# Storing the last five tiles of a log-softmax in transfers of unequal numbers of partitions

## The chip, the cores and the metric

Every run uses one core of a Trainium2 chip; the experiments ran on three chips, each beside the kernel before on the same chip. The metric is the device time of one execution in microseconds (us). All runs here are fast, with a granted clock of 1.0.

## The reference

```python
def setup_inputs():
    batch, seq, vocab = 16, 512, 50000
    return {"x": np.random.randn(batch, seq, vocab).astype(np.float32)}

def reference(x):
    max_x = np.max(x, axis=-1, keepdims=True)
    shifted = x - max_x
    log_sum_exp = np.log(np.sum(np.exp(shifted), axis=-1, keepdims=True))
    return (shifted - log_sum_exp).astype(np.float32)
```

1,638.4 MB are read and as many written.

## The kernel before

A tile is 16 rows of x, each cut into 8 pieces: 128 partitions of 6,250 floats (25,000 B). There are 512 tiles in 64 rounds of 8 buffers. SP loads a buffer when its earlier store has landed; VectorE takes the maximum, ScalarE the exponentials with their sums, VectorE subtracts in place, and ScalarE issues the store. "Tile 507" is buffer 3 of the last round, "tile 511" the very last.

```python
P = 128
NBUF = 8

def take(engine, sem):
    engine.wait_ge(sem, 16).then_inc(sem, -16)

# SP
for j in range(NBUF):
    sync.dma_start(out=bufs[j], in_=dram(xq, 0, j)).then_inc(landed[j], 16)
with sync.Fori(1, rounds) as q:
    for j in range(NBUF):
        take(sync, stored[j])
        sync.dma_start(out=bufs[j], in_=dram(xq, q, j)).then_inc(landed[j], 16)
for j in range(NBUF):
    take(sync, stored[j])

# ... VectorE: front(j) waits for landed[j], takes the maximum; back(j) sums and subtracts

# ScalarE
def back(q, j):
    subtracted.next(
        scalar.dma_start(out=dram(oq, q, j), in_=bufs[j])
    ).then_inc(stored[j], 16)

# ... round 0
with scalar.Fori(1, rounds) as q:
    last = q - 1
    for j in range(NBUF):
        log((j - 1) % NBUF)
        front(j)
        back(q if j else last, (j - 1) % NBUF)
    settle()
log(NBUF - 1)
back(rounds - 1, NBUF - 1)
```

## Time and profile before

| | before |
|---|---|
| time, median | 7614.19 us (7613.91 to 7614.76, 4 runs) |
| VectorE, ScalarE busy | 79%, 41% |
| DMA | 430 GB/s over the span; 432 in the middle, 373 in the last fortieth |
| last increment of the last store | 7611.20 us after the start of the trace |

The lines themselves stand in the prediction. "DMA share" is the busy time of the 16 DMA engines, "GB/s" what they moved; a packet is counted whole in the stretch in which it starts. Two more things come from the trace's own records and from no view: the durations of single DMA packets (one row of 25,000 B is one packet), and the times at which each engine adds its increment to the semaphore of a transfer. The spread of the 16 increments of one transfer shows how far apart the engines are; how late the last one is, I call the lag of the slow engine.

### The profile page before, as it was taken

To read this page: it belongs to the slowest core of one execution; us is meant where nothing else is said; L and a number is where in the kernel's file an instruction comes from. 1 tells how busy PE (TensorE), PEld (TensorE's weight loads), DVE (VectorE), ACT (ScalarE), POOL (GpSimd) and SP (SyncE) were. 2 spreads that over 40 slices of the span, in tenths; PEclk is the share of its full clock that TensorE was granted. 3 is DMA by queue.
4 is the path that set the end of the run, shared out by engine and by line. 5 is a ranking of instruction groups with operands and counts; after the bars stand their busy time and mean duration, and the time that the engine had idled before them with its cause. 6 is when DMAs were issued, how large, how long until landed. Compare 5 with 4: busy or idle time off the path is not lost. (4 is left out here: it accounts for less than half of the span.)

```text
span 7612.6 us, 13283 instructions
## 1 busy us (share of the span) xinstructions
DVE 6049.3 (79%) x5632; ACT 3113.4 (41%) x2561; POOL 0.2 (0%) x4
## 2 busy tenths in 40 slices
DVE  8777877777777778777787777877777877778777
ACT  4444444444444443444444444444444444444443
POOL 0000000000000000000000000000000000000000
DMA  9999999999999999999999999999999999999998
GB/s 425 432 432 432 432 432 432 432 432 432 432 432 433 432 432 433 432 432 433 432 432 433 432 432 432 432 433 432 432 433 432 432 432 432 432 432 432 432 432 373
DMA packets 147459, 3276.89 MB, mean 430 GB/s; under 512 B 16384, under 2 KB 16384, under 8 KB 16384
## 3 DMA queue, kind: packets, MB, share of 16 engines
q1 hardware_dynamic: 73728, 1638.43, 50.0%
q10 hardware_dynamic: 73728, 1638.43, 50.0%
q14 instruction: 3, 0.02, 0.0%
HBM read 1638.40 MB, written 1638.40 MB: 430 GB/s over the span
## 5 line engine op out<-in xcount | busy, mean ns | idle before, releaser
L144 DVE TENSOR_REDUCE own<-buf 128x1 f32<-128x6250 f32 x512 | 3411.7, 6663 | 1267.0 <-DVEq L43 1267.0
L179 ACT ACTIVATE dump<-buf,negmax 128x3125 f32<-128x3125 f32 x1024 | 2929.3, 2861 | 33.3 <-DVE negmax L140 16.8
L188 ACT ACTIVATE logsum<-total 128x1 f32<-128x1 f32 x512 | 103.8, 203 | 4447.9 <-DVE total L140 4447.9
L153 DVE TENSOR_SCALAR buf<-buf,negmax,logsum 128x6250 f32<-128x6250 f32 x512 | 1810.2, 3536 | 138.9 <-ACT logsum L188 138.9
L126 DVE STREAM_TRANSPOSE block<-own 128x32 f32<-128x32 f32 x1024 | 216.6, 212 | 35.1
L129 DVE TENSOR_REDUCE rowval<-block 128x4 f32<-128x32 f32 x1024 | 190.4, 186 | 35.4
L135 DVE COPY spread<-rowval 128x32 f32<-128x32 f32 x1024 | 185.5, 181 | 35.6
L179 ACT ACTIVATION_READ_ACCUMULATOR dump<-buf,negmax 128x1 f32 x1024 | 190.8, 186 | 0.0
L140 DVE STREAM_TRANSPOSE total<-spread 128x32 f32<-128x32 f32 x512 | 108.4, 212 | 17.7
L140 DVE STREAM_TRANSPOSE negmax<-spread 128x32 f32<-128x32 f32 x512 | 108.3, 212 | 17.7
L149 DVE TENSOR_REDUCE own<-part 128x1 f32<-128x2 f32 x512 | 57.5, 112 | 2.4 <-ACT dump L179 2.4
L200 ACT ACT_TABLE_LOAD x1 | 1.3, 1283 | 0.9 <-SPq L85 0.9
L231 POOL MEMSET const-bfloat16-1.0<- 128x1 bf16 x1 | 0.1, 102 | 0.0
L231 POOL MEMSET const-uint8-127<- 128x1 uint8 x1 | 0.1, 102 | 0.0
L231 POOL MEMSET const-float32-0.0<- 128x1 f32 x1 | 0.1, 99 | 0.2 <-issue 0.2
L231 POOL MEMSET const-float32-1.0<- 128x1 f32 x1 | 0.1, 99 | 0.0
## 6 DMA issues: line engine op xcount, KB each, us to landing
buf<-in_x_dram SPq DMA_DIRECT2D x512, 3125.0 KB, 55.5
out_dram<-buf ACTq DMA_DIRECT2D x512, 3125.0 KB, 35.7
```

What stands on the lines that cost most here:

```text
L126: vector.transpose(out=block32, in_=own.to_broadcast([P, SQ]))
L129: vector.tensor_reduce(out=rowval, in_=block32.rearrange("p (r g) -> p r g", g=G), op=op, axis=AX, negate=negate,)
L135: vector.tensor_copy(out=spread.rearrange("p (r g) -> p r g", g=G), in_=rowval[:, :, None].to_broadcast([P, SQ // G, G]),)
L140: on_dve.next(vector.transpose(out=out, in_=spread)).then_inc(done.sem)
L144: vector.reduce_max(out=own, in_=bufs[j], axis=AX).then_inc(on_dve.sem)
L149: vector.tensor_reduce(out=own, in_=parts[j], op=ALU.add, axis=AX)
L153: vector.tensor_scalar(out=bufs[j], in0=bufs[j], scalar1=shift[j][:, 0:1], scalar2=logs[j], op0=ALU.add, op1=ALU.subtract,)
L179: ins = scalar.activation(out=dump, in_=bufs[j][:, c * EXP_C : (c + 1) * EXP_C], func=ACT.Exp, bias=shift[j][:, 0:1], scale=1.0, accum_out ...
L188: scalar.activation(out=logs[j], in_=totals[j][:, 0:1], func=ACT.Ln)
L200: nc.scalar.preload_act_table_set("natural_log_exp_and_others")
L231: nc = _bacc.Bacc("TRN2", target_bir_lowering=False, num_devices=1)
```

## The change

The intent is to even out the end: one of the 16 DMA engines has fallen behind, so the last five tiles are cut into transfers that should give it less, and others more. ScalarE's last round is taken out of its loop so that its stores can differ.

```diff
+SPLIT = (120, 8)
+STEPS = (*range(2, 16), 9)
+
+def groups(j):
+    return STEPS if j == NBUF - 1 else SPLIT if j >= NBUF - 5 else (P,)
+
-def take(engine, sem):
-    engine.wait_ge(sem, 16).then_inc(sem, -16)
+def take(engine, sem, n=16):
+    engine.wait_ge(sem, n).then_inc(sem, -n)
@@ SP
-            take(sync, stored[j])
+            take(sync, stored[j], 16 * len(groups(j)))
@@ ScalarE
-        def back(q, j):
-            subtracted.next(
-                scalar.dma_start(out=dram(oq, q, j), in_=bufs[j])
-            ).then_inc(stored[j], 16)
+        def back(q, j, groups=(P,)):
+            p = 0
+            for n in groups:
+                dst = dram(oq, q, j)
+                ins = scalar.dma_start(out=dst[p : p + n], in_=bufs[j][p : p + n])
+                if p == 0:
+                    subtracted.next(ins)
+                ins.then_inc(stored[j], 16)
+                p += n
+            assert p == P
@@
-        with scalar.Fori(1, rounds) as q:
+        with scalar.Fori(1, rounds - 1) as q:
             ...
+        for j in range(NBUF):
+            log((j - 1) % NBUF)
+            front(j)
+            back(rounds - 1 if j else rounds - 2, (j - 1) % NBUF, groups(j - 1))
         log(NBUF - 1)
-        back(rounds - 1, NBUF - 1)
+        back(rounds - 1, NBUF - 1, groups(NBUF - 1))
```

## The prediction

The forecast's sum, with all its terms: 7611.2 - 2.5 - 3.1 + 7.5 = 7613.1, and 3.0 more make 7616.1. The shares of packets (none of the last five tiles on engine 15; on engine 0 one more of tile 510 and fifteen of the last tile) were my assumption. A rival given 35% and 7622 to 7640 ("a time near 7640 at worst"): the packets of the last five stores take twice as long, 1.86 us.

The engines' numbers are labels of mine, as no record names an engine. I take it that the engines of a smaller transfer are always among those of a larger one, and call engine n the one that transfers on n + 1 engines have and those on n have not.

> **What bounds the kernel now.** I read the page first, then the stretches of the end, then the timeline of the end, then the trace's own records of DMA packets and of semaphore increments by DMA.
>
> The page says that the DMA engines are the bound, and that they are full until the last slice:
>
> ```profile
> DMA  9999999999999999999999999999999999999998
> GB/s 425 432 432 432 432 432 432 432 432 432 432 432 433 432 432 433 432 432 433 432 432 433 432 432 432 432 433 432 432 433 432 432 432 432 432 432 432 432 432 373
> q1 hardware_dynamic: 73728, 1638.43, 50.0%
> q10 hardware_dynamic: 73728, 1638.43, 50.0%
> buf<-in_x_dram SPq DMA_DIRECT2D x512, 3125.0 KB, 55.5
> out_dram<-buf ACTq DMA_DIRECT2D x512, 3125.0 KB, 35.7
> ```
>
> The reader is to see 512 loads and 512 stores of 128 rows of 25,000 B, and two queues whose packets fill the 16 engines together. One row is one packet of 928 ns, and each engine has 512 x 8 x 2 = 8,192 of them. VectorE is 79% busy, ScalarE 41%; neither sets the pace. Only the last slice falls, so I cut the end into stretches (columns: stretch, length, busy VectorE, ScalarE, GpSimd, clock, DMA share, GB/s):
>
> ```profile
> 7400.00:7500.00 100.00, 80.10 (x77) 38.51 (x34) 0.00 (x0) 1.00 1.00 432
> 7500.00:7580.00 80.00, 62.22 (x57) 35.31 (x29) 0.00 (x0) 1.00 0.83 358
> 7580.00:7594.00 14.00, 11.29 (x11) 5.90 (x5) 0.00 (x0) 1.00 0.50 214
> 7594.00:7613.00 19.00, 4.48 (x6) 0.38 (x3) 0.00 (x0) 1.00 0.70 299
> ```
>
> Against 432 GB/s the last three lose 13.7, 7.1 and 5.8 us of all 16 engines, some 27 us together. Why engines idle there is in the semaphore increments: each transfer makes 16, one for each engine. In the second round of eight tiles the last of a load's 16 comes 0.8 us after the ninth; in round 8 it is 3 us, in round 33 13 us, in the last round 32 us, while the other fifteen stay within 4 us. So **one engine is 0.4% slower** (32 of 7,600 us) and has fallen about 34 packets behind. In the last 60 us that engine alone still loads: the last tile's load has landed on the first engine at 7545.2 and on the slow one at 7579.34. The timeline shows what hangs on it:
>
> ```profile
> 7564.57 6.66 DVE L144 TENSOR_REDUCE own<-buf 128x1 f32<-128x6250 f32 x1 [2.49 <-DVEq L43]
> ...
> 7573.40 3.54 DVE L153 TENSOR_SCALAR buf<-buf,negmax,logsum 128x6250 f32<-128x6250 f32 x1 [0.27 <-ACT logsum L188]
> ...
> 7579.47 6.66 DVE L144 TENSOR_REDUCE own<-buf 128x1 f32<-128x6250 f32 x1 [2.54 <-DVEq L43]
> ...
> 7591.87 0.34 ACTq L193 DMA_DIRECT2D out_dram<-buf  x1
> ...
> 7599.13 0.35 ACTq L193 DMA_DIRECT2D out_dram<-buf  x1
> ```
>
> The reader is to see that the maximum of the last tile waits for a load (DVEq L43) by 2.54 us only, and that the last two stores are issued 12.4 and 19.7 us after it starts. Of the last store's increments fifteen come by 7608.14 and the last at 7611.20, because the slow engine drains 8 packets of each of the last stores one behind the other. The time is 3.0 us later (7614.2).
>
> [...]
>
> **The change part by part.** The last round leaves ScalarE's loop; the same work is done, and ScalarE is idle most of the time: 0 us. [...] Engine 15 loses all 40 packets of its last five stores, which is the lag of 34 and a bit more. I take it that it is the slow one, since the change is cut to fit that.
>
> *Earlier last load.* The slow engine alternates loads and stores until its loads are done. Store 506 is not changed and lands on it at 7568.14. From 7567.7 six load packets remain; now they come without stores between them, ending at 7567.7 + 6 x 0.93 = 7573.3 instead of 7577.9. That is 4.6 us, but VectorE is busy with the tile before until 7576.94 (7573.40 + 3.54), so the last maximum starts there and not at 7579.47: **2.5 us gained**. The last two stores are issued at 7589.4 and 7596.6.
>
> *The laggard's tail.* The slow engine no longer ends 3.1 us after the others: **3.1 us gained**, to the fast engines' 7608.1.
>
> *The crooked last tile.* Engine 0 has 1 packet more of tile 510 and 15 instead of 8 of the last: 8 x 0.934 us = 7.5 us, all on the path, since nothing stands behind it: **7.5 us lost**. Checked from the start: store 510's data starts 0.85 us after its issue (as 7592.72 follows 7591.87), 7590.2; 9 packets to 7598.6; 15 more at 0.934 to 7612.6; increment 0.45 us later, 7613.1.
>
> *Issues.* 18 more of 0.34 us on ACT's queue; the last fifteen take 5.1 us from 7596.6, while engine 0 needs one each 0.93 us. Hidden.
>
> Sum: 7611.2 - 2.5 - 3.1 + 7.5 = 7613.1, and with the 3.0 us after it a time of **7616.1**: two packets slower than before.
>
> **The rivals.** [...] *Another engine is slow.* If it is one of 0 to 7 [...]the lag grows: 7619 to 7625. For it: the packets have no number. *The pieces spread evenly.* If the small transfers rotate over the engines, 128 rows are 8 each again, the 7.5 us fall away, and the two gains stay: about 7609.[...]
>
> **Range and chances.** I give the bare count of packets (7616) 45%,[...] a wrong slow engine 8%, the gain 12%. Half of the weight lies below some 7619, and 8 in 10 between 7611 and 7636. 2% is 152 us; not even the worst case comes to a third of that.
>
> **What would show it.** 530 store issues; packets up by 140, all semaphore writes. The maximum of the last tile at 7577 with almost no wait for its load shows the first step. Increments of the last store spread over 13 us, the last near 7613, show the third.[...] A last increment before 7609 would prove the shares wrong; a maximum of the last tile still at 7579.5 or later would mean that engine 15 is not the slow one.

## The result, and the profile after

| | before | after |
|---|---|---|
| time, median | 7614.19 us (4 runs) | 7642.08 us (7641.68 to 7643.06, 4 runs) |
| ratio | | 1.0037, 95% interval 1.0019 to 1.0054 |
| last store issued | 7599.13 | 7605.47 (first of fifteen) |
| last increment of the last store | 7611.20 | 7639.89 |
| store packets from the first store of the last five (7547.5) on: mean, share over 1.1 us | 934 ns, 0% | 1,608 ns, 68% |

The ratio is the mean time of the fast runs of one kernel over that of the other's of the same rounds, so not quite the ratio of the medians. The 28 us are far outside the scatter of both.

The page after, the DMA's rows and queues and three of the issue rows (columns of an issue row: count, KB each, us to landing):

```profile
DMA  9999999999999999999999999999999999999998
GB/s 425 432 432 432 432 432 432 432 432 432 432 432 432 432 433 432 432 432 432 432 432 433 432 432 432 432 433 432 432 432 432 432 432 433 432 432 432 432 432 308
q10 hardware_dynamic: 73868, 1638.43, 50.2%
q1 hardware_dynamic: 73728, 1638.43, 49.8%
out_dram<-buf ACTq DMA_DIRECT2D x507, 3125.0 KB, 35.7
out_dram<-buf ACTq DMA_DIRECT2D x4, 2929.7 KB
out_dram<-buf ACTq DMA_DIRECT2D x5, 195.3 KB
```

Only the last slice moved by more than 1 GB/s, from 373 to 308. The queue of the stores has 140 packets more, all semaphore writes, as predicted. The stretches of the end, cut as before, with one more for what is new (stretch, length, busy VectorE, ScalarE, GpSimd, clock, DMA share, GB/s):

```profile
7500.00:7580.00 80.00, 61.20 (x56) 33.00 (x28) 0.00 (x0) 1.00 0.91 341
7580.00:7594.00 14.00, 7.94 (x9) 1.79 (x2) 0.00 (x0) 1.00 0.92 229
7594.00:7613.00 19.00, 8.36 (x9) 6.28 (x6) 0.00 (x0) 1.00 0.74 179
7613.00:7642.00 29.00, 0.00 (x0) 0.00 (x0) 0.00 (x0) 1.00 0.51 118
```

The reader is to compare the last two columns with those of before. Between 7500 and 7580 the engines are busier (0.91 instead of 0.83) and move less (341 instead of 358 GB/s); between 7580 and 7594 they are 92% busy and move 229 GB/s, where full engines move 432. Busy and slow: the packets take longer, and the records of the packets say so (last row of the table).

The timeline of the end after the change (start, length, engine, line, what, and the idle time before with what ended it):

```profile
7567.09 6.66 DVE L154 TENSOR_REDUCE own<-buf 128x1 f32<-128x6250 f32 x1 [5.56 <-DVEq L53]
...
7585.81 6.67 DVE L154 TENSOR_REDUCE own<-buf 128x1 f32<-128x6250 f32 x1 [6.36 <-DVEq L53]
...
7598.21 2.26 ACTq L206 DMA_DIRECT2D out_dram<-buf  x2
...
7605.47 29.37 ACTq L206 DMA_DIRECT2D out_dram<-buf  x15
```

The maximum of the last tile starts at 7585.81, 6.3 us later than before and not 2.5 us earlier: its load landed at 7585.68 instead of 7579.34. The last store is then 6.3 us later (7605.47), and from its issue to its last increment it takes 34.4 us instead of 12.1. 6.3 + 22.3 is the whole of the 28.7 us.

The increments told at once that one premise was wrong. The two transfers of tile 507 make 25 increments. I read 15 and 8 of them as the engines', for the store queue has 140 writes of 4 B more than before, 4 x 7 for these tiles and 112 for the last one; the other two came at 7547.36 and 7547.93, before any data could be through (the next one came at 7555.81). All but two came by 7565.1; the two late ones came at 7587.55 and 7588.48, one packet apart. So the slow engine had a share in **both** the 120 and the 8 rows: by the numbering above it is one of 0 to 7, not 15.

### The profile page after: what moved, and what is told of

Read it like the earlier page. It is cut to its first block, busy times and chain, and to the rows that moved or that the text cites. A ratio compares the mean times of both kernels' runs of the same rounds, so it can differ in the third digit from the quotient of the medians.

```text
span 7641.3 us, 13278 instructions
## 1 busy us (share of the span) xinstructions
DVE 6050.7 (79%) x5632; ACT 3113.4 (41%) x2561; POOL 0.2 (0%) x4
## 5 line engine op out<-in xcount | busy, mean ns | idle before, releaser
L189 ACT ACTIVATE dump<-buf,negmax 128x3125 f32<-128x3125 f32 x1024 | 2929.2, 2861 | 33.1 <-DVE negmax L150 16.5
```

What stands on the lines that cost most here:

```text
L189: ins = scalar.activation(out=dump, in_=bufs[j][:, c * EXP_C : (c + 1) * EXP_C], func=ACT.Exp, bias=shift[j][:, 0:1], scale=1.0, accum_out ...
```

## The experiments

All outputs are right. Where two engines' order is told, it is from the increments.

**The change in parts.** Theory A: with these cuts packets of 0.93 us take 1.9, because of the rows that the engines read at the same time. Theory B: packets are not the cost, the many small issues on ScalarE's queue are. First ScalarE's unrolled round alone:

```diff
 def groups(j):
-    return STEPS if j == NBUF - 1 else SPLIT if j >= NBUF - 5 else (P,)
+    return (P,)
```

> ScalarE's last round outside the loop, every store whole (128 rows). All theories: nothing on the path changes, 7614 us within 1 us, last increment near 7611. If the restructured loop itself costs, the time would be some way towards 7642.

7614.44 us (2 runs), last increment 7611.31. The restructured loop costs nothing.

```diff
-    return STEPS if j == NBUF - 1 else SPLIT if j >= NBUF - 5 else (P,)
+    return SPLIT if NBUF - 5 <= j < NBUF - 1 else (P,)
```

> Only tiles 507 to 510 in 120 and 8 rows; the last tile whole. Theory A ([...]packets take 1.9 us): the last tile's load still lands 6 us late (7585.7), the last store is issued at 7605.5 but waits behind store 510, which ends at 7619.8, then 8 packets of 0.93 us: time about 7630. Theory B (the packets are not the cost, the many small issues of about 2 us each on ScalarE's queue are): the last store is one issue, so the last increment comes 12 us after it and the time is 7614 to 7621.

7630.68 us (2 runs): theory A. The timeline has the same late maximum as after the change, and a last store of a single short issue:

```profile
7585.49 6.66 DVE L153 TENSOR_REDUCE own<-buf 128x1 f32<-128x6250 f32 x1 [6.44 <-DVEq L52]
...
7605.15 0.36 ACTq L205 DMA_DIRECT2D out_dram<-buf  x1
```

The late load comes from the splits, then, and its last store still ends only at 7627.23, because tile 510 in front of it ends at 7619.79.

```diff
-    return STEPS if j == NBUF - 1 else SPLIT if j >= NBUF - 5 else (P,)
+    return STEPS if j == NBUF - 1 else (P,)
```

> Only the last tile in 2 to 15 and 9 rows, all others whole. Theory A: store issue as before the change at 7599.1, engine 0 has 15 packets of 1.9 us, some 29 us: time 7630 to 7633. Uneven shares alone (15 packets of 0.93 us): 7619 to 7622. Theory B: fifteen issues of 2 us give the same 7630 to 7633, but packets of 0.93 us.

7631.63 us (2 runs), last increment 7628.62, 17.4 us later than before. The maximum is where it was before, the issues are long:

```profile
7579.54 6.66 DVE L153 TENSOR_REDUCE own<-buf 128x1 f32<-128x6250 f32 x1 [2.49 <-DVEq L52]
...
7599.19 24.66 ACTq L205 DMA_DIRECT2D out_dram<-buf  x15
```

The packets from that issue on had a mean of 1,834 ns, 73% over 1.1 us. Shares alone (15 packets of 0.93 us) would have given 7619 to 7622. The two parts cost 16.5 and 17.4 us by themselves and 27.9 together; some 6 us are shared, presumably because the first pieces of the last tile wait for tile 510 anyway.

**Equal shares, other rows.** The decisive question is whether the long packets come from the unequal shares, from small transfers, or from which partitions are read together. Three kernels store the last tile alone in other ways, all other tiles whole:

```diff
+PIECES = tuple(slice(16 * i, 16 * i + 16) for i in range(8))                         # last_block16
+PIECES = tuple(slice(i, P, 8) for i in range(8))                                     # last_comb16
+PIECES = tuple(slice(h + r, h + 32, 4) for h in range(0, P, 32) for r in range(4))   # last_comb8
-                ins = scalar.dma_start(out=dst[p : p + n], in_=bufs[j][p : p + n])
+                ins = scalar.dma_start(out=dst[rows], in_=bufs[j][rows])
```

> Last tile in 8 transfers of 16 neighbouring rows: each engine gets 8 packets as before, so shares are equal. Theory A[...]:[...] packets of some 3.7 us, last tile 7.4 us -> up to 30 us, fewer if the engines drift apart: time 7625 to 7637. Theory shares: equal shares, 7614. Theory B (number of issues): as last_comb16.

> Last tile in 8 transfers of 16 rows, every eighth row: same number of issues, same rows and same equal shares as last_block16[...]. Theory A: packets of 1.86 us, last tile 15 us: time 7619 to 7624, clearly less than last_block16. Theory B: the same as last_block16.

> Last tile in 16 transfers of 8 rows, every fourth row of a group of 32: more and smaller transfers than either, only engines 0 to 7, 16 packets each[...]. Theory A: packets stay at 0.93 us and 16 of them take 15 us, time 7620 to 7623 (7.5 us above before, all of it share). Theory B (16 issues of 2 us): 7631 or more.

The 3.7 and 1.86 us in these expectations are four and two times 0.93. The packets measured are in the table and below it.

| kernel | transfers x rows | engines, packets each | rows of one transfer | packets from the last tile's first issue on: median, share over 1.1 us | time |
|---|---|---|---|---|---|
| before | 1 x 128 | 16, 8 | all | 935 ns, 0% | 7614.2 |
| last_comb8 | 16 x 8 | 8, 16 | every fourth of 32 | 935 ns, 2% | 7617.1 and 7621.7 |
| last_comb16 | 8 x 16 | 16, 8 | every eighth | 1,891 ns, 89% | 7618.8 (2 runs) |
| last_block16 | 8 x 16 | 16, 8 | neighbours | 2,008 ns, 82% | 7622.0 (2 runs) |

last_comb16 and last_block16 give every engine the same eight rows' worth as before, and still cost 4.6 and 7.8 us. last_comb8 has twice as many and smaller transfers and its packets are those of before. So neither the shares nor the smallness makes the long packets, but which rows are read together. The stretches from 7600 to 7610 of the three, in the order last_block16, last_comb16, last_comb8 (the last two columns are DMA share and GB/s):

```profile
7600.00:7605.00 5.00, 0.00 (x0) 0.00 (x0) 0.00 (x0) 1.00 0.64 120
7605.00:7610.00 5.00, 0.00 (x0) 0.00 (x0) 0.00 (x0) 1.00 0.90 195
```

```profile
7600.00:7605.00 5.00, 0.00 (x0) 0.00 (x0) 0.00 (x0) 1.00 1.10 245
7605.00:7610.00 5.00, 0.00 (x0) 0.00 (x0) 0.00 (x0) 1.00 0.98 245
```

```profile
7600.00:7605.00 5.00, 0.00 (x0) 0.00 (x0) 0.00 (x0) 1.00 0.49 205
7605.00:7610.00 5.00, 0.00 (x0) 0.00 (x0) 0.00 (x0) 1.00 0.48 200
```

The reader is to see half of the engines moving 200 GB/s in last_comb8, and all of them busy for 245 in last_comb16. (Counting a packet where it starts gives the share of 1.10; it also gives last_block16 only 0.64 in its first stretch, since its first packets start just before 7600.) For last_block16 I had expected packets of 3.7 us and 7625 or more. The first fifteen packets of last_block16 did take 3.1 to 3.8 us (median 3.6), near four times the usual 0.93. After them the starts of the engines spread out, only 5 more packets were over 3 us, and the time was 7622. So the factor was right while the engines were in step, the time was expected too high, and the order of the three was right.

One confusion has to be named: neighbouring partitions hold neighbouring rows of DRAM too, so these kernels also change the distance of the addresses written. Closeness in DRAM alone does not explain the table, since the rows of last_comb16 lie 200 KB apart and those of last_comb8 100 KB, and the wider ones are the slow ones.

The trace of split_only tells more. When the 120 rows of tile 509 start at 7579.9, fourteen engines take them up (the slow one is still at tile 508). Twelve of the first fourteen packets take 1.6 to 2.0 us and two take 0.93, and it is the same with the next fourteen and in the trace after the change. If each engine has eight neighbouring rows, all fourteen lie alike in DRAM, and still two packets are not longer; that does not fit the distance in DRAM either. That engines have eight neighbouring rows each stays an assumption, as no record names an engine or a row, and what the engines share when their packets get longer is not shown.

The runs of last_comb8 differ by 4.7 us: in the profiled one the slow engine ended store 510 at 7598.78 instead of some 7603.7. One run of the kernel before, beside the first four experiments, also took 7609.37 instead of 7614. I did not find out why; the packets are the reading here.

The long issues go with the long packets. The rows of ScalarE's issues in the last stretch, before, after and in last_comb8 (ns min/median/max):

```profile
L193 ACTq DMA_DIRECT2D out_dram<-buf x1: 354/354/354, 7599.1 to 7599.1; - x1
```

```profile
L206 ACTq DMA_DIRECT2D out_dram<-buf x16: 242/2040/2602, 7598.6 to 7632.2; - x16
```

```profile
L205 ACTq DMA_DIRECT2D out_dram<-buf x16: 642/859/1235, 7595.1 to 7608.8; - x16
```

An issue right behind another takes about as long as a packet of the engines that it goes to: 2.0 us where packets take 1.9, 0.86 where they take 0.94, 0.35 where none was just before. So the length of an issue follows the packets; a fixed cost of 2 us for each, as theory B has it, is ruled out by last_comb8.

**Which engine is slow.** The slow engine's increment is late in each transfer that it has a share in, so the number of late increments among transfers on few engines tells its number, as defined beside the prediction.

```diff
+WHO = (112, 7, 6, 3)      # who_is_slow; (112, 7, 5, 4) in who_is_slow2
 def groups(j):
-    return STEPS if j == NBUF - 1 else SPLIT if j >= NBUF - 5 else (P,)
+    return WHO if j == 1 else (P,)
```

> Tile 505 alone in 112, 7, 6 and 3 rows, while the slow engine lags by some 17 us in the stores.[...] one late increment (the 112 rows alone) means a slow engine numbered 7 or more, two mean 6, three mean 3 to 5, four mean 0 to 2. The trace after the change had two late increments in each of the 120 and 8 row stores, so the slow one is among 0 to 7, not 15 as I predicted[...]. Time 7613 to 7620.

> Tile 505 in 112, 7, 5 and 4 rows. who_is_slow had three late increments (7554.49, 7557.26, 7560.05, nothing else after 7548), so the slow engine is 3, 4 or 5. Here two late increments mean 5, three mean 4, four mean 3.

The last increments of tile 505 were 7547.05, 7547.91, then 7554.49, 7557.26, 7560.05 in the first and 7546.71, 7547.07, then 7553.66, 7556.44, 7559.21 in the second. Three late ones each, 2.8 us apart: in the transfers of 112, 7 and 6 rows but not 3, and of 112, 7 and 5 but not 4. That is **engine 4** (counted from 0), on that chip. Times 7617.19 and 7617.37: this one tile cost 3 us.

**Can relief pay at all?** If the time is the slow engine's own sum of packets, taking eight from engine 4 in the middle of the run should save 7.4 us. All these kernels start from the kernel before and cut only buffer 0's store in some rounds (`segments()` gives the rounds before FIRST, those from FIRST to LAST - 1, which are cut, and the rest; SP waits for as many more increments there):

```diff
+CUT = 5470
+PIECES = (
+    (slice(0, P), slice(0, CUT)),
+    (slice(0, 124), slice(CUT, None)),     # relieve8; in relieve_control one
+    (slice(124, P), slice(CUT, None)),     # piece (slice(0, P), slice(CUT, None))
+)
+FIRST, LAST = 30, 38
-        with scalar.Fori(1, rounds) as q:
+        for lo, hi, pieces in segments():
+            with scalar.Fori(lo, hi or rounds) as q:
                 ...
-                back(q if j else last, (j - 1) % NBUF)
+                    back(q if j else last, (j - 1) % NBUF, pieces if j == 1 else WHOLE)
```

> The kernel before, but in the middle of the run (rounds 30 to 37) one tile of eight is stored as 5,470 of 6,250 columns of all 128 rows, and the other 780 columns as 124 and 4 rows, which run on four engines[...]. who_is_slow2 had three late increments, so the slow engine is number 4: it is relieved of one packet of 0.93 us in each of 8 tiles. If the time is the slow engine's own sum of packets, the time falls by 8 x 0.93 = 7.4 us to about 7607 (7605 to 7609). If the slow engine is another, or the end is set by the order of the last stores, 7614 or more. Engines 0 to 3 get 24 packets more, some 22 us, less than the 32 us lag.

> The same cut at column 5,470 in the same 8 tiles, but the 780 columns go as 128 rows on all 16 engines: no shift of shares. If relieve8 gains by shares, this stays at 7614 within 1 us; if cutting a store in two gains or costs by itself, it shows here.

relieve8 took 7627.2 us (7625.03 to 7629.31, 4 runs), relieve_control 7613.55 (7613.12 to 7613.71, 4 runs) beside 7614.46 of before (7 runs). The expectation of relieve8 fell, but not cleanly. Its GB/s row shows that all engines lost time in the middle:

```profile
GB/s 424 432 432 432 432 432 432 432 432 432 432 432 432 432 432 432 432 432 432 432 430 428 421 424 432 432 432 432 432 432 432 432 432 432 431 432 432 431 431 380
```

Four slices fall short of 432 by 25 together, about 11 us of a slice of 190. Engines alternate between a load and a store packet: the first short store packets, of 0.124 us, start 1.05 us apart on an engine, which leaves just the 0.93 us of a load packet between them. So 32 of them on engines 0 to 3 took 32 turns, and their stores fell behind. The loss in the middle did not reach the end: twelve engines end by 7608.0, where fifteen ended by 7608.1 before. Four end later, at 7614.4 to 7622.1. In the last round these four lag by 37 to 46 us in the stores but by only 5 to 8 us in the loads, and the engine that lags most in the loads, by 13.7 us, is among the twelve. (Which increments belong together can be told: an engine that has done its loads stores its eight rows of a tile in about 7.5 us, one that still loads in about 14.8.) So the slow engine was no longer the last; the four that had its work were. The expectation had called their 22 us "less than the 32 us lag".

The control is the more telling one. Cutting the stores in two on all engines moved the slow engine's lag from the loads to the stores: in the last round its load of buffer 4 landed 4.3 us behind the first engine instead of 33.9, but its store of buffer 0 37 us behind the fifteenth engine instead of 17. The end shows what that was worth. Before, then relieve_control:

```profile
7560.00:7580.00 20.00, 14.43 (x13) 10.47 (x9) 0.00 (x0) 1.00 0.55 234
7580.00:7600.00 20.00, 15.77 (x17) 6.28 (x6) 0.00 (x0) 1.00 0.63 270
7600.00:7613.00 13.00, 0.00 (x0) 0.00 (x0) 0.00 (x0) 1.00 0.59 252
```

```profile
7560.00:7580.00 20.00, 14.84 (x17) 7.92 (x8) 0.00 (x0) 1.00 0.93 401
7580.00:7600.00 20.00, 1.45 (x1) 0.00 (x0) 0.00 (x0) 1.00 0.50 214
7600.00:7613.00 13.00, 0.00 (x0) 0.00 (x0) 0.00 (x0) 1.00 0.05 19
```

VectorE is done 17.6 us earlier and fifteen engines end by 7590.5 instead of 7608.1, but one engine goes on alone (a share of 0.05 is less than one of 16) to 7610.36, 0.84 us before the end of the kernel before. Its work is a fixed sum; ordering it otherwise moves the idle time of the others and not the end.

Two kernels then cut one single tile by whole rows:

```diff
# rows only; all columns
+PIECES = (slice(0, 116), slice(116, P, 3), slice(117, P, 3), slice(118, P, 3))   # skip4
+PIECES = (slice(0, 125), slice(125, P))                                           # load4
+FIRST, LAST = 32, 33
```

> The kernel before, but one tile of 512 (round 32, first buffer) is stored as 116 rows[...] and 3 transfers of 4 rows: 32 rows on each of engines 0 to 3, none on the others. Whole rows, so no small packets that hold up the stores as in relieve8[...]. If the slow engine is number 4 and the time is the sum of its packets, it has 8 packets less: 7.4 us, time about 7607 (7604 to 7610). If the slow engine is one of 0 to 3, 24 more: 7630 to 7637. If the lag is not what sets the time: 7614.

> The same tile as 125 rows[...] and 3 rows: 25 rows on each of engines 0 to 4 (one more on 0 to 2), none on the others. If the slow engine is number 4, it has 17 packets more: +15.8 us, time about 7630 (7627 to 7633). If it is 5 or higher, it is relieved of 8 and the time is about 7607 as in skip4; skip4 and load4 differ by what engine 4 gets.

skip4 took 7628.17 us (7620.34 to 7647.27, 4 runs), load4 7634.03 (7632.47 to 7636.27, 4 runs), before 7614.33. The cut store of skip4 took from 3818 to 3892, twice its usual time, with 111 packets over 1.1 us between 3840 and 3900; the next load of that buffer waited for it, and in round 33 the loads of buffer 4 began to land 9.3 us later than in the kernel before. The end of the profiled run shows what became of it. Twelve engines end by 7608.9 and four at 7614.4 to 7617.2. In the last round one engine lags by 15.5 us in the load of the last tile (34.1 before) and by 3.3 in the stores; its lag has grown from at most 7.5 us in round 33, so it is the slow one. Four others lag by only 4 to 7 us in the loads, but by 32 to 37 us in the stores. They are as many as had been given 24 packets more, and they are the four that end last. So skip4 fell as relieve8 did: the slow engine was relieved, and engines 0 to 3 set the end. Its expectation had named 24 packets more only for the case that one of these was the slow one.

load4 was expected at 7627 to 7633 for engine 4 and lay 1 us above: two engines ended at 7628.7 and 7629.3, fourteen at 7612.3. Why there were two I do not know. The loads of round 32, just after the cut store, tell the number again. In skip4, where four engines had more to store, five of buffer 4's load increments come 5.6 to 18.6 us after the first, the other eleven within 0.5. In load4, where five had more, it is again five (5.5 to 18.3), the others within 0.7. So the slow engine, the one at over 18 us, is none of 0 to 3 and one of 0 to 4: it is engine 4 on this other chip too.

The last pair spreads the relief over eight tiles:

```diff
+PIECES = (slice(0, 112), *(slice(112 + i, P, 4) for i in range(4)))   # gentle4
+PIECES = (slice(0, 112), slice(112, P))                               # gentle_control
+FIRST, LAST = 30, 38
```

> Eight tiles (one of eight in rounds 30 to 37) stored as 112 rows on all 16 engines (7 each) and four transfers of 4 rows, every fourth row, on engines 0 to 3. Engine 4 has one packet less in each, engines 0 to 3 three more, so a store ends only some 6 us later and no buffer is held for long, unlike in skip4, whose one store held its buffer 38 us longer and stalled all engines for 14.7 us. If the time is the slow engine's own sum and the slow one is number 4: 8 x 0.93 = 7.4 us less than gentle_control, and about 7607 to 7609. If relief never pays, the same as gentle_control or more.

> The same 112 rows, and the other 16 rows in one transfer on all 16 engines, so each has 8 packets as before. It carries the cost of the unnatural order of rows[...] without a shift of shares: 7614 to 7618.

Both were far off: 7649.76 us (7641.60 to 7654.87) and 7657.48 (7653.25 to 7668.25), 4 runs each, before 7614.29. The control shows that 112 and 16 rows, with equal shares, cost 43 us for eight tiles, over 5 us a tile. Between 3900 and 4020 it had 121 of 1,953 packets over 1.1 us and 407 GB/s, where 432 is usual. With the relief it was 7.7 us less, near the 7.4 expected, but the runs of each spread over 13 to 15 us, and in the trace of gentle4 four engines again end after the other twelve, by up to 13.4 us. So a gain by relief is not shown.

No experiment gave a version worth having: relieve_control is 0.9 us, 0.01%, below before.

## Why the prediction was wrong

- **What bounds the kernel now** held: a single DMA engine 0.4% slower than the others, and the end waits for it. relieve_control shows it best. "About 34 packets behind" was too many: in the last round the loads lag by 32 us but the stores by 17, and an engine that does both gives each one packet in 1.86 us (mostly so far apart start the loads on the slow engine at the end, while it also stores), so I now estimate 17 loads and 9 stores, 26 packets.
- **"I take it that it is the slow one"**, of engine 15, was wrong, and this is the first failed step. I took the number from the cut of the change, although the packets of the trace before carry no number, as the prediction says itself. It is engine 4. So *Earlier last load* (2.5 us gained) and *The laggard's tail* (3.1 us gained) could not happen: engine 4 keeps 8 packets of each 120-row transfer and one of each 8-row transfer, 9 instead of 8, in four tiles (two late increments in each of the stores 507 to 509), and by its number 12 in the last one, as twelve of the fifteen transfers there have 5 rows or more. Measured instead: the last load 6.3 us later. split_only shows that the splits alone do this; even the unchanged store 506 ended on engine 4 at 7574.54 instead of 7568.14.
- **The crooked last tile** had the right mechanism for its shares and the wrong size: 15 packets on engine 0 (steps_only has room for 16 in its 29.4 us), but of 1.83 us on the mean in steps_only and not 0.934. The term of 7.5 us measured 17.4 in steps_only. This is the second failed step. It was a term I could have put into the sum, for packets of 1.86 us stood in my text, and I left them to a rival.
- **Issues: hidden** held in substance. They took 2 us each and not 0.34, but last_comb8 shows that they follow the packets.
- **ScalarE's unrolled round, 0 us** held (peel_only).
- **The rival of the long packets** was what happened as far as the packets go: near the 1.86 us that it named (of those over 1.1 us after the change the median is 1.90). What makes them long is not shown. I gave it 35% and at worst "a time near 7640"; it came to 7642.1. This worst case left the last tile at 14 us, that is at 0.93 us a packet, against its own 1.86; from the end of tile 510 (7619.81) to the end of the last store it took 20.1. And I set the upper end of the range at 7636, inside that rival's own span. With 35% on 7622 to 7640, an upper end that left out its worst part was too tight.
- **What would show it** was well chosen: the two signs named against the main line, long packets in the last five tiles and a maximum of the last tile at 7579.5 or later, both appeared.

Left open: why one engine is slower, what makes the packets long, and whether relieving the engine can pay. relieve8 and skip4 did relieve it, at the price of four others that ended later still. It would need a transfer that leaves out engine 4, spreads its rows over more than four engines, keeps the packets at 0.93 us and does not lengthen the store; the cuts that I tried each lacked one of these.

## What to carry to other kernels

A store of all 128 partitions is worth more than its byte count: cut by partitions, the last tile had packets of 1,891 ns as the median where every eighth row went together (last_comb16), and at first of 3.6 us where neighbours did (last_block16), instead of 935 ns, even with an equal share for every engine. Before moving work off a slow engine, find its number by experiment (the late increments of small transfers tell it), judge a lag by what the slow engine's own sum would be without it, not by how long the others idle, and look who ends last after the relief: it can be the engines that took over the work. In the profile, compare the DMA share with the GB/s: here 0.92 with 229 GB/s meant long packets (after, 7580 to 7594), and 0.50 with 214 missing work (before, the same stretch).
